# All sixteen gate pairs by seven products: the first pair's operands and sums made in another order and by other engines

## The chip, the cores and the metric

The kernel runs on one core of one Trainium2 chip. The metric is the time that the device takes for one launch, in microseconds; shown is the median of several runs. A profile of one execution shows what each engine of the core did: TensorE (PE in the profile), VectorE (DVE), ScalarE (ACT), GpSimd (POOL) and SyncE (SP), and PEld, TensorE's loading of weights, which overlaps its matmuls. ACT and DVE compute, POOL here mostly starts data transfers (DMAs) and adds a little, SP only starts transfers.

## The reference, cut to what matters

One layer of a hybrid model is computed for 640 tokens (512 of a sample, 128 of a prompt) of width 1024, all in fp32. The part that the change touches is the gated sum of four mixers:

```python
    proj = h @ lw['w_in']
    ...
    y_a = a_b * dwconv3(a_c * a_x, lw['conv_a_w'], lw['conv_a_b'])
    y_b, s_f, s_b = hgrn2_bidir(b_q, b_ff, b_fb, b_i, b_g, ...)
    y_c = ... neighbourhood_attention(qh, kh, vh, ctx_k, ctx_v, lw['na_rpb'])   # prompt: plain attention
    y_d = chunk_gmlp(d_u, d_v, lw['gmlp_norm_g'], lw['gmlp_ws'], lw['gmlp_b'])
    g_a, g_b, g_c, g_d = jnp.split(jax.nn.sigmoid(h @ lw['w_gate'] + lw['b_gate']), N_BRANCH, axis=-1)
    merged = (g_a * (y_a @ lw['w_br_a']) + g_b * (y_b @ lw['w_br_b'])
              + g_c * (y_c @ lw['w_br_c']) + g_d * (y_d @ lw['w_br_d']))
    return merged @ lw['w_o'], kh, vh, s_f, s_b
```

`h` is 640 x 1024, each `y` is 640 x 256, `w_gate` is 1024 x 4096 and each `w_br` 256 x 1024. After it come the norm and a feed-forward part of width 2816 with a short convolution.

## The kernel before, in words

**Numbers.** An fp32 operand is kept as two rounded parts, a high one (made by ACT, a copy that rounds) and a low one (made by DVE, the operand less its high part). A product is three matmuls: high by high, high by low, low by high. Features lie on the 128 partitions and tokens on the free axis, in two halves of 320 columns (`HC`), so that the matmul of most of the program is 128 x 128 by 128 x 320.

**Stages.** In this order: the modulation vectors, the input projection tile by tile, and, mixed into its matmuls, the mixers d (gMLP), b (HGRN), a (convolution) and c (attention); then the gate stage; then `w_o`, the norm, the feed-forward's up part and its down part.

**Who goes when.** The mixers and the preparation of operands are generators ("jobs"). Each `yield x` puts the job off by x of a clock that advances with the matmuls placed (`tick`), so numbers such as those in the list `HD` set how far one step of a mixer stands from the next in PE's row. `drain(f)` runs the jobs until `f` holds. Within an engine, instructions then go in the order in which they were placed; an instruction that waits holds up all behind it. From `g_all` on that order is fixed by hand (`omm`, `oact`, `ovec`, `opool` are PE, ACT, DVE and POOL with the order kept). Most such instructions have one line in the profile, that of the helper that records them (L151 before, L150 after), so they are told apart by their tiles.

**The gate stage.** It has 32 output tiles, four mixers by eight tiles of 128 features. Tiles n and n+4 of a mixer make a pair. A pair is a product of a 2 x 2 arrangement of weight blocks with a 2 x 2 arrangement of `h` (feature halves by token halves), and can be done in two ways. Plain (`gate_tile`): each tile has 48 matmuls by `h` and 12 by `y`, 120 for the pair. By seven products (Strassen's scheme, in the form with few sums): `gprod(o, p, i)` is product i, 12 matmuls, `bprod` its counterpart on `y`, 3 matmuls; 7 x 12 + 7 x 3 = 105 for the pair. Products 1 to 4 take the four quarters of `h` (kept in XH, XL0, XL1), products 5, 6 and 7 sums and differences of the quarters (kept in X1, X0 and F in some order). The weights of the seven are called A (products 1, 2), B (5, 6), Z (7) and C (4, 3); B, Z and a part of C are sums of blocks, made by DVE from two loads of `w_gp` (`raw`, and `G` or `raw`). Every operand, sum or not, has to be split into high and low. Some products add onto the bank of an earlier one, so that DVE or ACT must have taken the earlier value out before.

Before the change the first pair (mixer d, tiles 0 and 4) is plain, and the fifteen others go by seven products (`g_pair`). While the two plain tiles run on PE, the jobs make the `h` sums, the sums of the first seven-product pair's weights and their splits; the attention runs to its end in the same stretch.

**Names the steps use.** `m` and `g` are PSUM banks; `ga`, `gb` the two gates' partial sums; `y` the partial sums of the products by `y`; `g_split` splits an `h` sum, `g_zh` and `g_zl` are the high and low part of Z; `y_sums` and `y_split` make the sums of a mixer's `y` quarters and split them; `gp_load` starts the two loads of a pair's weights; `hss` are small row sums of the HGRN norm, to which POOL applies a power; `usum` and `wsum` are sums of feed-forward weights that POOL forms with accumulating transfers in DRAM, all through the middle of the program.

## Time and profile before

| | |
|---|---|
| median of 3 runs | 997.26 us (997.17 to 997.35) |
| profiled execution, its own time | 997.34 us |
| its span, first to last instruction | 995.5 us |
| mean granted TensorE clock | 0.998 |
| PE busy | 984.3 us, 7452 instructions |
| DVE busy | 864.0 us |
| ACT busy | 588.4 us |
| POOL busy | 186.6 us |
| first pair by seven products starts | 291.55 us |

The page gives the busy time of each engine over the span; the chain of waits gives, for the work that ended last, the engine on which each stretch of it lay. Rows of the timeline read: start, duration, engine, line, operation, output <- inputs, shapes, count, and in brackets the idle time before the row and what ended it. A row "x12" is twelve instructions in a row. The clock is the share of full speed that was granted to TensorE.

### The profile page before, as it was taken

Reading aid. Unit: us, or ns where it says so; the run is one execution under the profiler, and the core shown is the slowest. Engines: PE = TensorE matmul, PEld = TensorE weight load, DVE = VectorE, ACT = ScalarE, POOL = GpSimd, SP = SyncE. Lnnn points to the kernel's source line nnn. Section 1 sums busy time; section 2 is a strip of 40 time slices with the busy share of each in tenths; the row PEclk is TensorE's granted clock in tenths of the full one; section 3 lists DMA queues with packets and bytes.
Section 4 is the critical chain, followed back from the end, with each engine's and each line's share of the span. In section 5 each row is a group of like instructions: output and inputs, shape, how many; then the busy total and the mean of one; then the engine's idle time right before and its main releaser. Section 6 shows DMA issues by size and latency. Waiting matters only on the chain.

```text
span 995.5 us, 18982 instructions
## 1 busy us (share of the span) xinstructions
PE 984.3 (99%) x7452; PEld 933.1 (94%) x7452; DVE 864.0 (87%) x1413; ACT 588.4 (59%) x1018; POOL 186.6 (19%) x251
## 2 busy tenths in 40 slices
PE   8999999999999999999999999999999999999997
PEld 6899999999999999999998899999999999888886
DVE  6679899878799889898878688999999998999796
ACT  6652343455566565555656377877777777756672
POOL 1000020313112130342320021322222222100004
PEclk9999999999999999999999999999999999999999
DMA  9887343499466898999999684766666666976842
GB/s 353 338 282 249 127 134 123 133 266 273 107 223 171 235 226 291 272 225 295 290 249 367 217 324 134 221 172 167 177 170 163 177 170 193 367 262 211 288 129 106
DMA packets 74281, 220.99 MB, mean 222 GB/s; under 512 B 10192, under 2 KB 25328, under 8 KB 71504
## 3 DMA queue, kind: packets, MB, share of 16 engines
q1 hardware_dynamic: 44544, 150.96, 43.1%
q0 software_dynamic: 29648, 68.82, 29.8%
q8 instruction: 58, 0.95, 0.4%
q14 instruction: 31, 0.25, 0.1%
HBM read 176.74 MB, written 54.80 MB: 233 GB/s over the span
## 4 chain that ended last, share of the span: by engine, by line
PE 95%; DVE 2%; DMA 2%; POOL 1%; issue 1%; SPq 0%; POOLq 0%; ACT 0%
PE m L151 22%; PE g L1670 21%; PE g L375 14%; PE m L2133 9%; PE m L1670 5%; PE g L151 5%; PE m L1432 4%; PE g L2133 4%; PE g L950 2%; PE g L1432 1%; PE m L539 1%; PE m L1665 1%; DMA A<-in_w_ada_dram 1%; PE m L879 1%; POOL hss L318 1%; PE m L950 1%
## 5 line engine op out<-in xcount | busy, mean ns | idle before, releaser
L375 PE MATMUL g<-XH,w 128*128 128x320 f32 x640 | 155.0, 317 | 0.0
L375 PEld LDWEIGHTS g<-XH,w 128*128 128x128 f32 x640 | 109.5, 188 | 2.5 <-issue 1.2
L375 PE MATMUL g<-XL,w 128*128 128x320 f32 x320 | 98.8, 309 | 0.0
L151 PE MATMUL m<-XH,w 128*128 128x320 f32 x400 | 94.7, 311 | 0.0
L151 PEld LDWEIGHTS m<-XH,w 128*128 128x128 f32 x400 | 68.1, 188 | 1.2 <-ACT XH L151 0.6
L151 PE MATMUL m<-XL,w 128*128 128x320 f32 x200 | 60.6, 310 | 0.0
L375 PEld LDWEIGHTS g<-XL,w 128*128 128x128 f32 x320 | 60.3, 188 | 0.0
L2133 PE MATMUL m<-w,XH 128*128 128x512 f32 x246 | 58.5, 390 | 0.0
L2133 PEld LDWEIGHTS m<-w,XH 128*128 128x128 f32 x246 | 46.1, 188 | 9.6
L151 ACT ACTIVATE w<-raw 128x640 fp32r<-128x640 f32 (+3 forms) x54 | 49.8, 938 | 5.4 <-PE g L375 2.2
L151 DVE TENSOR_TENSOR w<-raw,w 128x640 fp32r<-128x640 f32 (+3 forms) x46 | 47.0, 1039 | 1.3 <-ACT w L151 1.2
L151 POOL DMA_DIRECT2D wsum<-in_w_dn_dram x36 | 37.0, 1211 | 48.7 <-issue 34.3
L151 PE MATMUL m<-X,w 128*128 128x320 f32 x264 | 42.3, 309 | 0.0
L151 DVE SCALAR_TENSOR_TENSOR X<-X,p2t,X 128x641 f32<-128x641 f32 x44 | 38.9, 884 | 0.9
L151 PEld LDWEIGHTS m<-X,w 128*128 128x128 f32 x264 | 39.6, 188 | 0.0
L151 DVE SCALAR_TENSOR_TENSOR X<-MG,p2t,X 128x641 f32<-128x641 f32 x44 | 38.9, 883 | 0.8
L1670 PE MATMUL g<-XL,w 128*128 128x320 f32 x240 | 38.7, 310 | 0.1
L1670 PE MATMUL g<-XL,C 128*128 128x320 f32 x240 | 38.3, 309 | 0.0
L151 PEld LDWEIGHTS m<-XL,w 128*128 128x128 f32 x200 | 37.1, 188 | 0.6 <-issue 0.6
L151 ACT ACTIVATE gb<-m 128x320 f32<-128x320 f32 x30 | 13.1, 438 | 40.7 <-PE m L151 40.7
L1670 PEld LDWEIGHTS g<-XL,w 128*128 128x128 f32 x240 | 35.9, 188 | 1.0 <-ACT MG L2030 0.5
L1670 PEld LDWEIGHTS g<-XL,C 128*128 128x128 f32 x240 | 36.0, 188 | 0.0
(611 smaller groups left out, 2864.8 us busy)
## 6 DMA issues: line engine op xcount, KB each, us to landing
wsum<-in_w_dn_dram POOLq DMA_DIRECT2D x30, 512.0 KB, 11.8
raw<-in_w_gp_dram SPq DMA_DIRECT2D x23, 640.0 KB, 6.5
raw<-in_w_up_dram SPq DMA_DIRECT2D x28, 512.0 KB, 5.0
raw<-in_w_in_dram SPq DMA_DIRECT2D x19, 512.0 KB, 4.4
H<-in_w_adt_dram SPq DMA_DIRECT2D x19, 512.0 KB, 4.0
G<-in_w_up_dram SPq DMA_DIRECT2D x12, 512.0 KB, 5.2
raw<-wsum SPq DMA_DIRECT2D x12, 512.0 KB, 5.5
actx<-X POOLq DMA_DIRECT2D x22, 256.0 KB, 4.9
```

Of the source, the lines that this page charges most:

```text
L151: r = f(*args, **kw)
L318: pool.tensor_tensor(out, out, neghalf[:, 0:n], ALU.pow)
L375: mm(o, w[:, h, k0 + k, :], r(k)[:, s], start=(k == 0 and i == 0), stop=(k == kt - 1 and i == 2))
L539: mm(m[W * g:W * g + W, (i - s0) * W:(i - s0 + 1) * W], lhs, rhs, start=True, stop=True, tile_position=(64 * par, W * g))
L879: mm(mo[64 * hh_:64 * hh_ + 64, 0:P], v, ptt[(u + hh_) % 4][:, j * P:(j + 1) * P], start=(j == 0), stop=(j == 2))
L950: mm(o, x(kx)[:, ts], w[:, h, k, :], start=(kx == 0 and i == 0), stop=(kx == 7 and i == 2))
L1432: mm(m, mh[MHN[q]][:, hx, k % 2, t * P:(t + 1) * P], wo[q][:, hw, k % 2, :], start=(k == 0 and i == 0), stop=(k == 7 and i == 2))
L1665: mm(o, w[:, k, :], x[:, k, :], start=(first and not part and k == 0 and j == 0), stop=(part == 1 and k == 3), skip_group_check=True)
L1670: z = mm(o, w[:, k, :], x[:, k, :], start=(first and k == 0 and j == 0), stop=(k == 3 and j == 2), skip_group_check=True)
L2133: mm(ps, s[t // 4][:, hx, k, o:o + P], w[:, hw, k, c0:c1], start=first, stop=i == 2 and bi == len(batch) - 1 and k == len(ks) - 1, skip_gr ...
```

## The change

All sixteen pairs go by seven products; the plain `gate_tile` and its weight tensor are dropped. A new `g_pair0` writes out the first pair's products and everything that ACT, DVE and POOL do among them, including the preparation of pair 1. To have operands ready at that time, other work moves:

- The `h` differences are made earlier, one pace apart, and the `h` sums are split into F (product 6), X1 (5) and X0 (7) as the attention lets go of those tiles; the attention's spare tiles move to other places.
- The sums of the first two pairs' weight blocks are no longer made by DVE: POOL forms them in a DRAM tensor `gsum` with twelve transfers of 320 KB, six of them accumulating, right after the HGRN state copies. The operands are then loaded from `gsum` by SP (pair 0) and POOL (pair 1).
- The gMLP's output is also stored to DRAM by POOL (`ydd`) and loaded back by SP into G, where DVE makes its sums.
- The attention's steps stand 0.9 less apart in placed matmul time (`HD[11]`), its transposed-probability copies all go to ACT, the bias reloads and the store of the result go to POOL.
- The second half of pair 1's weights is loaded into G late, by POOL, when G is free of the `y` sums.
- The merged tiles take region C in place of MG1, and the `y` operands the reverse.

```diff
-HD = [4, 5, 2.1, 7, 2.2, 1.4, 1.5, 5, 2.0, 2, 11]
+HD = [4, 5, 2.1, 7, 2.2, 1.4, 1.5, 5, 2.0, 2, 11, 0.9]
...
-NPL = 1
...
+        pool.dma_start(ydd, yt)
...
         vw = x0[:, 0:1792]
-        spt = [x0[:, 1792:2560], x1[:, 0:768]]
+        pb = region("MG1", [P, 2560])
+        spt = [x0[:, 1792:2560], pb[:, 1536:2304]]
         sps4 = [spt[i // 2][:, 384 * (i % 2):384 * (i % 2) + 384] for i in range(4)]
-        eb = [x1[:, 768:1152], x1[:, 1152:1536]]
-        mk = x1[:, 1536:2304]
-        ktk = x1[:, 2304:2560]
-        pb = region("MG1", [P, 2560])
+        eb = [x1[:, 0:384], x1[:, 384:768]]
+        mk = x1[:, 768:1536]
+        ktk = bm[:, 512:768]
...
-                    nc.sync.dma_start(eb[hh_], a["rpbe"][2 + hh_])
+                    pool.dma_start(eb[hh_], a["rpbe"][2 + hh_])
...
-            copy(ptt[u % 4], m[:, 0:384], hh_)
+            act(ptt[u % 4], m[:, 0:384], AF.Copy)
...
-            mo = pm()
+            mo = R["mo"] if "mo" in R else pm()
...
+            else:
+                R["last"] = True
+            yield HD[6] + HD[8] + HD[11]
         s3(14)
-        nc.sync.dma_start(o_ck[0, 0].rearrange("h s d -> s h d"), ktk.rearrange("p (h d) -> p h d", h=4))
-        nc.sync.dma_start(ycd, yc.bitcast(F32))
+        opool.dma_start(ycd, yc.bitcast(F32))
...
-    def gate_tile(bi, n, w):
-        br = BR[bi]
-        ps = pg()
-        gemm(ps, w, 0, 8, xhk, xlk)
-        gt = gp.tile([P, T], F32, tag="gt", name=nm("gt"))
-        gc = C_BG + GI[br] * 8 + n
-        act(c2(gt), ps[:, :, 0:HC], AF.Sigmoid, bias=p1[:, gc:gc + 1])
...
-            yield 10
+        a21, a22, a11 = d[:, 0], d[:, 1], g
+        for x, h, c in ((a21, 0, 1), (a22, 1, 1), (a11, 0, 0)):
+            yield 4
             nc.sync.dma_start(x, hdr[h, c])
-        while "scores" not in R or "ada39" not in R:
+        yield 6
...
+            yield 6
...
+        def place(i, x, t):
...
+        while "r" not in gx:
+            yield 0.5
+        r = gx["r"]
+        s = gw[0, "S"] = [gp.tile([P, 5, P], F32, tag="gt", name=nm("s")) for i in range(2)]
+        for i in range(2):
+            nc.sync.dma_start(s[1 - i], gsum[0][:, 1 - i])
+        g_s23(0, r)
+        while "ab0" not in R:
+            yield 0.5
+        lows = g_c(0, r)
+        low(*lows[0])
+        while "ab1" not in R:
+            yield 0.5
+        b = gw[0, "B"] = gunit(0, 1)
+        for i in range(2):
+            oact(b[:, 0, 1 - i], s[1 - i], AF.Copy)
+        low(b[:, 1, 1], s[1], b[:, 0, 1])
+        while "scores" not in R:
+            yield 0.5
+        place(6, a11, "F")
+        R["gx3"] = True
+        yield 1
+        place(5, a22, "X1")
+        low(b[:, 1, 0], s[0], b[:, 0, 0])
+        yield 0.5
+        ovec.tensor_tensor(a22, a12, a11, ALU.add)
+        g_zh(0, r)
+        gx["t3"] = a22
+        gx["Y"] = a11.rearrange("p a t -> p (a t)")
+        y_load(0)
+        low(*lows[1])
+        while "yc" not in R:
+            yield 0.5
+        place(7, a21, "X0")
+        gx["Y1"] = a21.rearrange("p a t -> p (a t)")
...
+        if bi == 0:
+            nc.sync.dma_start(gx["Y"], ydd)
+            return
...
+    gsum = dram.tile([2, P, 3, 5, P], F32, name="gsum")
...
+        if p_ != 1:
+            gp_load2(p_, r)
+        return r
+    def gp_load2(p_, r):
+        if p_ > 1:
+            nc.sync.dma_start(r[1], gp_raw(p_, 1))
+        else:
+            eng = opool if p_ else nc.sync
+            eng.dma_start(r[1][:, 0], gp_raw(p_, 1)[:, 0])
+            eng.dma_start(r[1][:, 1], gsum[p_][:, 2])
...
+        if p_ == 1:
+            opool.dma_start(gx["S"], gsum[1][:, 0:2])
+            return
...
+    def g_pair0(r):
+        gx["bi"] = 0
+        bank = [pm() for i in range(4)]
+        R["mo"] = bank[2]
+        b1, b3, b2, b4 = [m[:, 0:HC] for m in bank]
+        ga = gw[0, "gt", 0] = gp.tile([P, T], F32, tag="gt", name=nm("ga"))
+        gb = gw[0, "gt", 1] = gp.tile([P, T], F32, tag="gt", name=nm("gb"))
+        ps = gw[0, "ps"] = pg()
+        p1_, p3_ = ps[:, 1, 0:HC], ps[:, 0, 0:HC]
+        gprod(b1, 0, 1, True)
+        oact(ga[:, 0:HC], b1, AF.Copy)
+        bprod(p1_, 0, 1, True)
+        oact(p3_, p1_, AF.Copy)
+        gprod(b4, 0, 4, True)
+        gprod(b3, 0, 2, True)
+        ovec.tensor_tensor(ga[:, 0:HC], b3, ga[:, 0:HC], ALU.add)
+        g_sig(0, 0, ga[:, 0:HC], ga[:, 0:HC])
+        bprod(p3_, 0, 2, False)
+        gprod(b1, 0, 6, False)
+        oact(gb[:, 0:HC], b1, AF.Copy)
+        drain(lambda: "t3" in gx)
+        g_split(3, gx["t3"])
+        g_s01(1, r[1])
+        drain(lambda: "Y1" in gx)
+        gprod(b2, 0, 5, True)
+        g_zl(0, r[0])
+        g_a(1, r[1])
+        gprod(b1, 0, 7, False)
+        oact(gb[:, HC:T], b1, AF.Copy)
+        y_sums()
+        ovec.tensor_tensor(ga[:, HC:T], b4, gb[:, HC:T], ALU.add)
+        g_sig(0, 0, ga[:, HC:T], ga[:, HC:T])
+        ovec.tensor_tensor(gb[:, HC:T], b2, gb[:, HC:T], ALU.subtract)
+        gx["C"] = region("MG1", [P, 2, 3, HC], F32R)
+        lows, x3 = y_split()
+        oact(x3[2], x3[1], AF.Copy)
+        for x in lows + [x3]:
+            low(*x)
+        gp_load2(1, r[1])
+        g_al(1, r[1])
+        gprod(b2, 0, 3, False)
+        y = gw[0, "y"] = gp.tile([P, T], F32, tag="gt", name=nm("y"))
+        c2_ = gw[0, "b2"] = pm()[:, 0:HC]
+        bprod(p1_, 0, 6, False)
+        oact(y[:, 0:HC], p1_, AF.Copy)
+        bprod(c2_, 0, 5, True)
+        ovec.tensor_tensor(gb[:, 0:HC], b2, gb[:, 0:HC], ALU.subtract)
+        bprod(p1_, 0, 7, False)
+        oact(y[:, HC:T], p1_, AF.Copy)
+        ovec.tensor_tensor(y[:, HC:T], c2_, y[:, HC:T], ALU.subtract)
+        late = []
+        g_b(1, late)
+        g_s23(1, r[1])
+        late += g_c(1, r[1])
+        r[2] = gp_load(2)
+        g_zh(1, r[1])
+        for x in late:
+            low(*x)
+        gx["Y"] = gx["Y1"]
...
-        drain(lambda: "gx3" in R)
+        drain(lambda: "gx3" in R and "last" in R)
...
+        g_pair0(r)
+        for p_ in range(1, GPAIR + 1):
+            for _ in range(5):
...
+        while "stc" not in R:
+            yield 1
+        for o, h, i, add in ((0, 0, 0, 0), (2, 1, 0, 0), (0, 1, 1, 1), (2, 1, 1, 1), (1, None, 0, 0), (1, 1, 0, 1)):
+            for p_ in range(2):
+                bi, n = gp_id(p_)
+                g = gsum[p_][:, i] if h is None else gp_raw(p_, h)[:, i]
+                z = pool.dma_start(gsum[p_][:, o], g, accum_op=ALU.add) if add else pool.dma_start(gsum[p_][:, o], g)
+                tc.keep_in_program_order(z)
+                yield 0.7
```

The table of instructions that results differs at three places that matter below.

**PE, from the first pair's end of product 1 to pair 1's second product.** Before, with product 2's last matmul, then 6, b2, 5, 7, b6, b5 (`m_358` is the bank of products 1, 6, 7 and 4, `m_364` that of 5 and 3):

```order
L151 MATMUL m_359_3726<-XH_14_256,w_334_3519 128x320
L151 MATMUL m_358_3725<-X0_346_3642,w_349_3664 128x320 x12
L151 MATMUL g_362_3743<-E_249_2778,w_334_3519 128x320 x3
L151 MATMUL m_364_3792<-X1_344_3625,w_349_3664 128x320 x12
L151 MATMUL m_358_3725<-F_339_3575,S0_351_3683 128x320 x12
L151 MATMUL g_362_3743<-C_357_3724,w_349_3664 128x320 x3
L151 MATMUL m_366_3819<-C_357_3724,w_349_3664 128x320 x3
```

After, with product 2's last matmul, then b2, 6, 5, 7 and the first two rows of product 3 (`m_341` is the bank of 1, 6 and 7, `m_343` that of 5 and 3):

```order
L150 MATMUL m_342_3581<-XH_14_258,w_313_3314 128x320
L150 MATMUL g_347_3586<-E_249_2793,w_313_3314 128x320 x3
L150 MATMUL m_341_3580<-F_339_3575,w_338_3571 128x320 x12
L150 MATMUL m_343_3582<-X1_348_3590,w_338_3571 128x320 x12
L150 MATMUL m_341_3580<-X0_350_3605,S0_349_3601 128x320 x12
L150 MATMUL m_343_3582<-XH_14_258,w_332_3488 128x320
L150 MATMUL m_343_3582<-XL0_15_259,w_332_3488 128x320
```

Product 3 has moved up to stand right behind product 7, on the bank that product 5 filled; products 6, 5 and 7 stand together, with b2 ahead of them; product 4 has moved ahead of product 2, and b6, b5 and b7 behind product 3; then pair 1's product 1 begins.

**DVE around the split of the second `h` quarter's low part (`XL0`) and the low part of Z (`S0`).** Before:

```order
L151 TENSOR_TENSOR S0_351_3683<-raw_310_3261,S0_351_3683 128x640
L151 TENSOR_TENSOR XL0_15_257<-D_269_2885,XH_14_256 128x4x320
L151 TENSOR_TENSOR ga_360_3727<-m_359_3726,ga_360_3727 128x320
L151 TENSOR_TENSOR D_269_2885<-D_269_2885 128x320 x4
```

After:

```order
L150 TENSOR_TENSOR ga_345_3584<-m_342_3581,ga_345_3584 128x320
L150 TENSOR_TENSOR XL0_15_259<-D_269_2901,XH_14_258 128x4x320
L150 TENSOR_TENSOR S0_349_3601<-raw_288_3058,S0_349_3601 128x640
L150 TENSOR_TENSOR G_270_2902<-G_270_2902 128x320 x4
L150 TENSOR_TENSOR ga_345_3584<-m_344_3583,gb_346_3585 128x320
L150 TENSOR_TENSOR gb_346_3585<-m_343_3582,gb_346_3585 128x320
```

The low part of Z now stands behind the low part of the `h` quarter, and the bank of product 5 (`m_343`) is taken out behind a sum that needs product 7 (`gb`).

**ACT in the first pair and at the start of pair 1.** After the change, from the first sigmoid to the copy of product 7 (the two rows `gb<-m_341` are the copies of products 6 and 7 out of their bank):

```order
L150 ACTIVATE ga_345_3584<-ga_345_3584,cst_81 128x320
L150 ACTIVATE gb_346_3585<-m_341_3580 128x320
L150 ACTIVATE XH_14_258<-D_269_2901 128x4x320
L150 ACTIVATE B_351_3674<-raw_340_3578 128x1280
L150 ACTIVATE gb_346_3585<-m_341_3580 128x320
```

The split of the `h` quarter (`XH<-D`) now stands behind the copy of product 6, where before it stood behind product 1's. Further on, up to the copy of pair 1's product 1 (`m_363<-m_362`):

```order
L150 ACTIVATE w_357_3737<-raw_340_3578 128x640
L150 ACTIVATE w_357_3737<-G_353_3703 128x640
L150 ACTIVATE S0_349_3601<-G_353_3703 128x640
L150 ACTIVATE gb_346_3585<-gb_346_3585,cst_81 128x640
L150 ACTIVATE m_363_3758<-m_362_3757 128x320
```

`G_353`, read by two splits ahead of `m_363`, is the half of pair 1's weights that POOL now loads late, where before SP had loaded it ahead of the pair.

158 lines of the change are left out of this document (44 added, 114 removed).

## The prediction

> **What bounds the kernel now.** I read the page first, then the chain of waits, then the busy time in stretches.
>
> ```profile
> PE 984.3 (99%) x7452; PEld 933.1 (94%) x7452; DVE 864.0 (87%) x1413; ACT 588.4 (59%) x1018; POOL 186.6 (19%) x251
> ...
> PE 95%; DVE 2%; DMA 2%; POOL 1%; issue 1%; SPq 0%; POOLq 0%; ACT 0%
> ```
> ```profile
> 200.00:300.00 100.00, 99.85 (x761) 94.23 (x760) 81.31 (x161) 54.10 (x100) 21.61 (x29) 1.00 0.75 218
> 300.00:400.00 100.00, 100.00 (x684) 100.00 (x683) 89.28 (x122) 60.02 (x98) 22.10 (x33) 1.00 0.80 231
> ```
>
> TensorE is busy 99% of the span, and 95% of the chain lies on it. In the stretch of the change (200 to 300 us) it idles 0.15 us in 100; between 300 and 400, all gate products, never. So two things follow. A matmul that goes is worth its full pitch, and there is no idle time to win beyond that. Any new wait on TensorE is lost in full, since nothing behind it has slack for it to be made up. The pitch: 684 matmuls in 100 us, 0.1462 us each.
>
> **What is removed.** The plain pair has 120 matmuls, seven products have 105. 15 x 0.1462 = 2.19 us. That is the most that the change can give: 997.34 (the profiled execution) - 2.19 = 995.15 us. DVE, ACT and POOL do about the same amount as before; nothing on the path gets shorter by it.
>
> **What is moved, around the first pair.** What hides the work of ACT and DVE is the run of matmuls in front of the product that needs it. Before, up to 291.55 us two plain tiles are that cover:
>
> ```profile
> 289.79 1.92 PE L375 MATMUL g<-E,w 128*128 128x320 f32 x12
> 291.55 0.31 PE L151 MATMUL m<-XH,w 128*128 128x320 f32 x1
> ...
> 293.57 0.44 ACT L151 ACTIVATE ga<-m 128x320 f32<-128x320 f32 x1 [0.45 <-PE m L151]
> ...
> 294.03 0.82 DVE L151 TENSOR_TENSOR S<-raw,S 128x640 fp32r<-128x640 f32 x1
> ...
> 294.34 1.26 ACT L151 ACTIVATE XH<-D 128x1280 fp32r<-128x1280 f32 x1
> ...
> 295.51 1.92 PE L151 MATMUL m<-X,w 128*128 128x320 f32 x12
> 295.64 1.49 DVE L151 TENSOR_TENSOR XL<-D,XH 128x1280 fp32r<-128x1280 f32 x1 [0.79 <-ACT XH L151]
> ...
> 297.27 0.60 PE L151 MATMUL g<-E,w 128*128 128x320 f32 x3
> ...
> 299.47 1.92 PE L151 MATMUL m<-F,S 128*128 128x320 f32 x12
> ...
> 301.23 0.60 PE L151 MATMUL g<-C,w 128*128 128x320 f32 x3
> 301.43 0.44 ACT L151 ACTIVATE gb<-m 128x320 f32<-128x320 f32 x1 [1.31 <-PE m L151]
> ...
> 302.53 0.48 DVE L151 TENSOR_TENSOR gb<-m,gb 128x320 f32<-128x320 f32 x1
> ```
>
> Twelve matmuls take 1.76 us (295.51 to 297.27), three 0.44. A copy out of a bank starts 0.20 us after the product's last matmul (301.23 to 301.43) and takes 0.44. The low part of Z (`S<-raw,S`, 0.82) is done at 294.85, 4.6 us ahead of product 7 (299.47). The split of the `h` quarter (`XH`, 1.26, then `XL`, 1.49) is needed only after product 7. After the change the plain tiles are gone: the first pair starts about 120 x 0.1462 = 17.5 us earlier, at 291.55 - 17.5 = 274.0, and the chains below stand closer to the products that need them. I call the end of product 6 E6.
>
> *Product 7.* It needs the low part of Z from its third matmul on. In DVE's new row that stands behind the low part of the `h` quarter, which waits for the quarter's high part on ACT, which stands behind the copy of product 6. So from E6: 0.20 + 0.44 (copy; the next starts some 0.04 early) + 1.26 (`XH<-D`) + 0.05 + 1.40 (the pitch of a DVE operation of 1.49) + 0.82 (`S`) + 0.08 = about 4.2 us. Cover: product 5 (1.76) and two matmuls (0.29), 2.05. TensorE waits **2.1 us**. All of it is from rows; the bounds are 1.8 and 2.5.
>
> *Product 3.* It adds onto product 5's bank, so it waits until DVE has taken that out. The subtraction stands behind the sum that uses the copy of product 7. From the end of product 7: 0.20 + 0.44 + 0.04 + 0.40 + 0.48 + 0.08 = 1.64 us, and not one matmul lies between. **1.65 us**; bounds 1.4 and 2.0. Before, products b6 and b5, the whole of product 4 and b7 lay between.
>
> *Small ones.* Product b2 waits for ACT's copy of b1's bank, delayed by the splits ahead of it: 0.18. Product b7 waits for the copy of b6 (0.20 + 0.44 + 0.08) with b5 (0.44) between: 0.26. Pair 1's product 1 waits for the low part of its weights, the last of DVE's row of splits: 0.3. Together **0.7**, bounds 0 and 1.5.
>
> **The late half of pair 1's weights.** POOL starts its two loads of 320 KB into G once DVE has read the last of the `y` sums there. ACT must split both (0.42 to 0.74 us each, rows like `w<-raw`), then compute a sigmoid of 640 (0.82), then copy pair 1's product 1, for which TensorE's next product waits. Times: E6 = 274.0 + 54 matmuls (7.9) + 0.55 (next paragraph) + 0.2 = 282.65; product 7 ends at 282.65 + 4.2 + 1.45 = 288.3, product 3 at 288.3 + 1.65 + 1.76 = 291.7; b6, b5, b7, product 1, and the nine matmuls before the wait bring TensorE to 296.7. After product 7 DVE and ACT have 0.2 + 0.44 + 0.4 + 0.5 for the gates, a sigmoid and then the three splits of `y`; G is free at about 292.2, and the second load is issued about 293.1. It lands L later; ACT then has 0.74 + 0.82 + 0.44, and TensorE goes on at 295.1 + L. The wait is L - 1.6. No load of this size from POOL is in the trace. The nearest:
>
> ```profile
> raw<-in_w_gp_dram SPq DMA_DIRECT2D x23, 640.0 KB, 6.5
> ...
> usum<-in_w_up_dram POOLq DMA_DIRECT2D x18, 256.0 KB, 10.2
> ...
> usum<-usum POOLq DMA_DIRECT2D x6, 256.0 KB, 5.7
> ...
> C<-F POOLq DMA_DIRECT2D x9, 256.0 KB, 3.4
> ```
> ```profile
> 290.00:295.00 5.00, 5.00 (x36) 5.00 (x35) 3.39 (x5) 3.58 (x6) 0.00 (x0) 1.00 0.92 305
> ```
>
> 3.4 us is a light load, 10.2 one among many others in flight. Here the DMA engines were 0.92 busy in the same stretch; after the change the next pair's loads go out at about this time too. I take 5.0, between 3.4 and the 6.5 of twice the size: a wait of **3.4 us**, bounds 1.8 and 8.6. [...]
>
> **The attention.** Its steps move 0.9 closer.
>
> ```profile
> 229.32 0.56 DVE L2311 COPY MG<-m 128x384 f32<-128x384 f32 x1 [0.53 <-PE m L862]
> ...
> 235.88 0.41 DVE L859 TENSOR_SCALAR X<-X,ast 128x384 f32<-128x384 f32 x1
> ```
> ```profile
> 270.51 1.48 DVE L1067 TENSOR_TENSOR D<-D 128x1280 f32<-128x1280 f32 x1
> 275.61 1.49 DVE L1067 TENSOR_TENSOR D<-G,D 128x1280 f32<-128x1280 f32 x1
> ```
> ```profile
> 230.00:260.00 30.00, 30.00 (x244) 27.80 (x241) 26.16 (x61) 13.55 (x31) 10.30 (x13) 1.00 0.79 214
> ```
>
> DVE has 3.84 us free between 230 and 260. Five steps take 4.5 us out of that; three differences of 1.4 come in (270 and later before), and up to eight copies of 0.56 go to ACT. 4.5 + 4.2 - 4.5 - 3.84 = 0.4. Following DVE's row step by step, its scaling (0.41) for the sixth pair of units ends at 260.15 while TensorE wants it at 259.6. I take **0.55**, bounds 0 and 1.5. Where TensorE waits there, 40 matmuls in front have already been used as cover.
>
> **The POOL sums** cost nothing:
>
> ```profile
> 146.17 2.24 POOL L572 COPY D<-st_in 64x128 f32<-64x128 f32 x4
> 187.23 1.01 POOL L318 TENSOR_TENSOR hss<-hss,neghalf 128x4 f32<-128x4 f32 x1 [38.81 <-DVE hss L317]
> ```
>
> POOL is idle from 148.4 to 187.2. Twelve transfers at 0.6 to 1.0 us of issue, and three waits for a landing in a row, each 5.7 (the accumulating `usum<-usum`), end by 148.4 + 10 + 17 = 175. With 10.2 each: 189, 2 us late, on a row that the chain of waits runs through. So 0, bound 2.
>
> **The sum.** -2.19 + 2.1 + 1.65 + 0.7 + 3.4 + 0.55 = +6.2. On the profiled execution 997.34 + 6.2 = 1003.5; the median of the runs is 0.08 below it, so about **1003.5 us**.
>
> **Rivals.**
> 1. *Only the matmuls count* (995.2 us). ACT and DVE would need to be 4 us ahead of what their rows give. DVE idles 1.6 of 5 us at 290, which is for it; the order of the instructions is against.
> 2. *The late load is early* (L under 2, or ACT not behind it): 1003.5 - 3.4 = 1000.1. For it: the queue of POOL is short there. Against: the busy DMA engines.
> 3. *The waits are half of what I say*, +2 against -2.19: 997.2, no change.
> 4. *The late load is the bound*, slower: L of 8 to 10 gives +9 to +11, 1006 to 1008.5.
> 5. *The clock falls.* If TensorE stands still long enough, its clock is taken down:
>
> ```profile
> 987.76 1.17 PE L2133 MATMUL m<-w,MG 128*128 128x192 f32 x9
> ```
> ```profile
> 991.00:991.50 0.50, 0.00 (x0) 0.00 (x0) 0.44 (x1) 0.44 (x1) 0.03 (x1) 1.00 0.65 254
> 991.50:992.00 0.50, 0.00 (x0) 0.00 (x0) 0.32 (x1) 0.28 (x1) 0.00 (x0) 0.71 0.00 0
> ```
>
> The last matmul ends at 988.93, and the clock falls about 2.9 us later. A wait of 3.4 us could do the same; if the clock needs as long to come back, 2.9 us at half speed lose 1.5: 1005.0 us. [...]
>
> **How the numbers follow.** The forecast 0.40 (1001.5 to 1005.5), rival 1 0.05, rival 2 0.20, rival 3 0.16, rival 4 0.11, rival 5 0.08. The range, 998.5 to 1007.5, leaves out rival 1, most of 3 and the upper part of 4, some 0.2. A change under 0.2% (2.0 us) cannot be told from none: faster 0.05, within 0.19 (rival 3 and a small part of 2), slower 0.76 (rival 2 falls mostly there, at 0.28%).
>
> **What would show it.** In the profile after: TensorE's first idle time within the gate stage, ended by DVE's `S` (2.1 us, in product 7), by DVE's `gb` (1.65, ahead of product 3) and by ACT's `m` behind `w<-G` (3.4); a lower busy share of TensorE between 255 and 300 and the same 100% later; 15 matmuls fewer. No `S` wait would mean that the order of DVE's row is not what it seems; a wait ended by `hss` that the POOL sums do cost. A faster kernel with these waits in it would mean that time is won in a place that I have not seen.

## The result, and the profile after

The change makes the kernel slower: 1005.70 us (median of 4 executions, 1005.43 to 1006.26) against 997.21 us of the kernel before on the same chip, a ratio of 1.0086 [1.0068, 1.0103]. The profiled execution took 1005.73 us, 8.4 us more than that of before; its span is 1003.8 us and its mean granted clock 0.995, where before it was 0.998.

The page, engines and chain of waits:

```profile
PE 987.3 (98%) x7437; PEld 934.4 (93%) x7437; DVE 864.7 (86%) x1413; ACT 592.6 (59%) x1034; POOL 195.5 (19%) x267
...
PE 90%; DVE 5%; DMA 2%; issue 1%; POOL 1%; ACT 1%; SPq 0%; POOLq 0%; DVEq 0%; ACTq 0%
```

The 15 matmuls are gone (7452 before, 7437 now), and yet TensorE's busy time rose by 3.0 us: the work has not grown, so some of it ran more slowly, and the granted clock below shows where. TensorE's share of the chain fell from 95% to 90%.

Busy time in stretches of 100 us (PE, PEld, DVE, ACT, POOL, then the granted clock, the share of the DMA engines and GB/s):

```profile
200.00:300.00 100.00, 94.17 (x701) 86.88 (x700) 80.23 (x160) 56.34 (x113) 24.03 (x34) 0.98 0.64 198
300.00:400.00 100.00, 99.81 (x670) 99.81 (x671) 84.41 (x114) 57.36 (x93) 26.02 (x36) 0.98 0.91 253
```

The damage is between 200 and 304 us: 5.9 us of idle time that were not there before (6.02 in the two rows, against 0.15), and a clock of 0.98 in both rows, which was 1.00. The 0.98 of the second row lies in its first four microseconds, as a finer view will show. What TensorE waited for there (total, times, longest, from the waits view of TensorE):

```profile
PE m L150 <- DVE S L150: 1.9, 1, 1.9
PE m L150 <- ACT m L150: 1.8, 1, 1.8
PE m L150 <- DVE gb L150: 1.7, 1, 1.7
```

These are the three waits that the prediction names. In time order on TensorE, where the last bracket is the idle time and what ended it:

```profile
280.93 1.92 PE L150 MATMUL m<-F,w 128*128 128x320 f32 x12
282.68 1.92 PE L150 MATMUL m<-X,w 128*128 128x320 f32 x12
284.44 0.46 PE L150 MATMUL m<-X,S 128*128 128x320 f32 x2
286.80 3.00 PE L150 MATMUL m<-X,S 128*128 128x320 f32 x10 [1.90 <-DVE S L150]
291.53 0.39 PE L150 MATMUL m<-XH,w 128*128 128x320 f32 x1 [1.74 <-DVE gb L150]
...
300.19 0.41 PE L150 MATMUL m<-XH,B 128*128 128x320 f32 x1 [1.84 <-ACT m L150]
...
303.30 2.21 PE L150 MATMUL m<-F,w 128*128 128x320 f32 x12
```

Products 6 and 5 run through (1.92 us as displayed for twelve, starts 1.75 apart). Product 7 does two matmuls, stops, and does its other ten in 3.00 us; at full clock ten show 1.73 (e5). On DVE, ACT and POOL the causes:

```profile
283.22 1.26 ACT L150 ACTIVATE XH<-D 128x1280 fp32r<-128x1280 f32 x1
```
```profile
284.51 1.49 DVE L150 TENSOR_TENSOR XL<-D,XH 128x1280 fp32r<-128x1280 f32 x1 [2.82 <-ACT XH L150]
285.92 0.82 DVE L150 TENSOR_TENSOR S<-raw,S 128x640 fp32r<-128x640 f32 x1
...
290.30 0.49 DVE L150 TENSOR_TENSOR ga<-m,gb 128x320 f32<-128x320 f32 x1 [1.58 <-ACT gb L150]
290.89 0.49 DVE L150 TENSOR_TENSOR gb<-m,gb 128x320 f32<-128x320 f32 x1
```
```profile
294.52 0.55 POOL L150 DMA_DIRECT2D G<-gsum  x1
```
```profile
G<-gsum POOLq DMA_DIRECT2D x1, 320.0 KB, 3.7
```
```profile
295.32 0.44 ACT L150 ACTIVATE y<-g 128x320 f32<-128x320 f32 x1 [0.81 <-PE g L150]
295.65 1.26 ACT L150 ACTIVATE w<-D 128x1280 fp32r<-128x1280 f32 x1
297.10 0.74 ACT L150 ACTIVATE w<-raw 128x640 fp32r<-128x640 f32 x1 [0.19 <-DVE raw L150]
297.75 0.72 ACT L150 ACTIVATE w<-G 128x640 fp32r<-128x640 f32 x1
298.38 0.72 ACT L150 ACTIVATE S<-G 128x640 fp32r<-128x640 f32 x1
299.00 0.81 ACT L150 ACTIVATE gb<-gb,cst 128x640 f32<-128x640 f32 x1
299.72 0.41 ACT L150 ACTIVATE m<-m 128x320 f32<-128x320 f32 x1
```

The low part of Z (`S`) ends at 286.74 and product 7 goes on at 286.80. The subtraction that frees product 5's bank ends at 291.38 and product 3 goes on at 291.53. The late load is issued at 294.52 and lands 3.7 us later, at 298.22. ACT splits it at 298.38, computes the sigmoid and makes the copy for which TensorE waits until 300.19. But ACT did not stand waiting for that load: from its copy of product b7 (`y<-g`, 295.32) on it works with one break of 0.19 us, and `S<-G` follows `w<-G` by 0.63 us, as closely as where a load has long landed (297.34 behind 296.71 in e1).

TensorE's busy time and the granted clock (the number behind the busy time), in stretches of 3.41 us laid where the clock changes:

```profile
283.46:286.87 3.41, 1.51 (x11) 1.00 0.19 77
286.87:290.28 3.41, 2.92 (x10) 0.50 0.68 203
290.28:293.69 3.41, 2.16 (x15) 1.00 0.45 182
293.69:297.10 3.41, 3.26 (x22) 1.00 0.54 168
297.10:300.51 3.41, 1.57 (x11) 1.00 0.89 245
300.51:303.92 3.41, 3.41 (x15) 0.50 1.03 300
```

Twice the clock is 0.50 for 3.41 us, from 286.87 and from 300.51, each time after 3.41 us in which TensorE was busy 44% (1.51 of 3.41) or 46% (1.57). After 63% (2.16) and 96% (3.26) it was 1.00. Neither wait is longer than 1.9 us.

### The profile page after: what moved, and what is told of

It reads as the page before. It is cut to its first block, busy times and chain, and to the rows that moved or that the text cites. A ratio compares the mean times of both kernels' runs of the same rounds, so it can differ in the third digit from the quotient of the medians.

```text
span 1003.8 us, 18999 instructions
## 1 busy us (share of the span) xinstructions
PE 987.3 (98%) x7437; PEld 934.4 (93%) x7437; DVE 864.7 (86%) x1413; ACT 592.6 (59%) x1034; POOL 195.5 (19%) x267
## 4 chain that ended last, share of the span: by engine, by line
PE 90%; DVE 5%; DMA 2%; issue 1%; POOL 1%; ACT 1%; SPq 0%; POOLq 0%; DVEq 0%; ACTq 0%
PE m L150 23%; PE g L1721 21%; PE g L374 11%; PE m L2184 8%; PE m L1721 5%; PE g L150 5%; PE m L1474 4%; PE g L2184 4%; PE g L955 2%; PE g L1474 1%; PE m L539 1%; PE m L1716 1%; DMA A<-in_w_ada_dram 1%; POOL hss L317 1%; PE m L955 1%
## 5 line engine op out<-in xcount | busy, mean ns | idle before, releaser
L374 PE MATMUL g<-XH,w 128*128 128x320 f32 x576 | 140.6, 318 | 0.0
L374 PEld LDWEIGHTS g<-XH,w 128*128 128x128 f32 x576 | 98.7, 188 | 2.4 <-issue 1.2
L150 PE MATMUL m<-XH,w 128*128 128x320 f32 x416 | 98.4, 311 | 1.7 <-DVE gb L150 1.7
L374 PE MATMUL g<-XL,w 128*128 128x320 f32 x288 | 89.0, 309 | 0.0
L150 PEld LDWEIGHTS m<-XH,w 128*128 128x128 f32 x416 | 70.8, 188 | 3.5 <-ACT ga L150 2.1
L150 PE MATMUL m<-XL,w 128*128 128x320 f32 x208 | 63.0, 310 | 0.0
L374 PEld LDWEIGHTS g<-XL,w 128*128 128x128 f32 x288 | 54.2, 188 | 0.1
L1721 PE MATMUL g<-XL,w 128*128 128x320 f32 x240 | 38.6, 310 | 0.0
L1721 PEld LDWEIGHTS g<-XL,w 128*128 128x128 f32 x240 | 36.0, 188 | 0.6 <-ACT MG L150 0.3
L150 PE MATMUL m<-X,S 128*128 128x320 f32 x192 | 32.3, 318 | 1.9 <-DVE S L150 1.9
L150 PE MATMUL m<-XH,B 128*128 128x320 f32 x128 | 31.9, 318 | 1.8 <-ACT m L150 1.8
```

The costliest lines, as they stand in the source:

```text
L150: r = f(*args, **kw)
L374: mm(o, w[:, h, k0 + k, :], r(k)[:, s], start=(k == 0 and i == 0), stop=(k == kt - 1 and i == 2))
L1721: z = mm(o, w[:, k, :], x[:, k, :], start=(first and k == 0 and j == 0), stop=(k == 3 and j == 2), skip_group_check=True)
```

## The experiments

Times are medians, with lowest and highest; ratios are to the kernel before, run between them on the same chip, whose median was 997.1 to 997.3 each time. The theory at the outset was the prediction's: three chains of ACT and DVE work stand too close to the products that need them. From the profile after came a second part: the waits also bring the clock down, to 0.50 behind two of the three. The reorderings keep the computation; where an experiment does extra work it is said. The executions of e1 to e3 lie 1.8 to 5.1 us apart and their intervals overlap, so their medians alone do not decide between theory and rival; there the rows of the profiled executions do.

### e1: the low part of Z made early

In the first pair's preparation instead of behind the split of the `h` quarter:

```diff
         low(*lows[1])
+        g_zl(0, r)
...
         gprod(b2, 0, 5, True)
-        g_zl(0, r[0])
```

> The low part of Z (DVE's S, 0.82 us) of the first pair is made earlier, right after its high part, instead of behind the low part of the h quarter (XL). Nothing else changes. In the changed kernel TensorE waits 1.9 us for it in product 7 (2.07 from the last matmul's pitch), and the granted clock then stands at 0.50 from 286.87 to 290.27, which costs product 7 another 1.4 us. Theory: the waits stand in a chain. Product 7 ends at 286.2 instead of 289.6, but DVE is then still at the y sums until 288.0, and the two operations ahead of product 3 end only at 288.9, so the wait there grows from 1.7 to about 2.7 us; with it TensorE is idle for more than half of the stretch 286.87 to 290.27, and the clock is down in the next such stretch. The late load keeps its wait of 2. Gain about 1.0 us: 1004.7. Rival (the waits are independent): the wait and the slow matmuls both go, 2.07 + 1.4 less: 1002.3.

Measured: 1004.05 us (1001.97 to 1005.88, 4), ratio 1.0068 [1.0049, 1.0087]. TensorE in its profile (span 1000.7):

```profile
289.16 0.60 PE L150 MATMUL m<-XH,w 128*128 128x320 f32 x1 [2.77 <-DVE gb L150]
...
299.15 0.41 PE L150 MATMUL m<-XH,B 128*128 128x320 f32 x1 [1.83 <-ACT m L150]
```
```profile
292.14 0.55 POOL L150 DMA_DIRECT2D G<-gsum  x1
```
```profile
294.28 0.44 ACT L150 ACTIVATE y<-g 128x320 f32<-128x320 f32 x1 [0.80 <-PE g L150]
...
297.34 0.72 ACT L150 ACTIVATE S<-G 128x640 fp32r<-128x640 f32 x1
```

The wait for `S` is gone, so DVE's order was its cause. But the wait for `gb` grew from 1.74 to 2.77, and the third is unchanged: 1.0 of the 1.9 us came back at the next place. The third wait also shows that the late load does not make it. The load was issued 2.38 us earlier than in after (292.14), took 3.6 us and landed at 295.74, 1.6 us before ACT read it, and TensorE still waited 1.83 us. From ACT's copy of product b7 to TensorE's restart there are 4.87 us in both kernels (294.28 to 299.15, 295.32 to 300.19): ACT's own row sets the wait, and it starts from a product of TensorE. The clock fell once in this execution (0.50 from 288.74 to 292.15, after a stretch with 1.06 of 3.41 us busy), not twice; at the end of the late wait the kernel is 1.04 us ahead of after, at its end 3.1.

### e2: product 5 taken out of its bank at once

DVE copies product 5 out, so that product 3 need not wait for the sum with product 7:

```diff
+        y = gw[0, "y"] = gp.tile([P, T], F32, tag="gt", name=nm("y"))
+        ovec.tensor_copy(y[:, HC:T], b2)
...
-        ovec.tensor_tensor(gb[:, HC:T], b2, gb[:, HC:T], ALU.subtract)
+        ovec.tensor_tensor(gb[:, HC:T], y[:, HC:T], gb[:, HC:T], ALU.subtract)
```

> Product 5's value is copied out of its bank by DVE during product 7 (one more DVE operation of some 0.5 us, into a part of y that is free), and the difference that stood between product 7 and product 3 reads the copy. So product 3 no longer waits for ACT's copy of product 7 and two DVE operations; 1.9 us from product 7's end to product 3's start go away there. Theory (chain): product 6's counterpart on y then waits for the split of the y sums, which ends at the same time as before (DVE's MG at 292.7), so 1.2 of it come back at once, and the rest is lost at the late load, whose landing (298.2) and the ACT row behind it set the restart at 300.2 as before: no gain, 1005.6. Rival (independent waits): 1003.8.

Measured: 1004.20 us (1003.39 to 1005.15, 4), ratio 1.0070 [1.0055, 1.0085]. In its profile the wait for `gb` is gone, and the late wait ends where it did:

```profile
300.06 0.42 PE L150 MATMUL m<-XH,B 128*128 128x320 f32 x1 [1.78 <-ACT m L150]
```

300.06 against 300.19: of 1.74 us, 0.13 was kept in this execution. The span is 0.4 shorter than that of after (this execution took 1005.15 us, the longest of the four). So the three waits are not three independent costs. What sets the restart here is a chain that begins at the end of product 7 and goes through the splits of `y` and of pair 1's weights on ACT and DVE, beside product 3 and not through it. The load adds at most 0.15 us to it: it lands at 298.1, and `S<-G` starts 0.78 us behind `w<-G` in place of 0.63. (The median, 1004.20, lies nearer to the rival's 1003.8; two of the four executions, 1003.39 and 1004.36, have a mean clock of 0.999, the profiled one 0.995, so the clock is mixed into it.)

### e3: ACT's copies ahead of the splits

Pair 1's C and Z are split behind ACT's copies, not ahead of them:

```diff
-        late += g_c(1, r[1])
         r[2] = gp_load(2)
-        g_zh(1, r[1])
...
         oact(p3_, p1_, AF.Copy)
+        if not q:
+            c_lows = g_c(1, r[1])
+            g_zh(1, r[1])
```

> ACT's splits of pair 1's C weights and Z (w<-raw, w<-G, S<-G, 2.2 us, two of them behind the late loads) and their DVE counterparts are placed behind ACT's copies of pair 1's first products instead of ahead of them. TensorE's second product of pair 1 then waits for a sigmoid and a copy only. Theory: the restart moves from 300.2 to about 298.2, and with TensorE busy from 297.1 to 300.5 the clock stays at 1.00 after it, which saves the 1.6 us that product 2 and the next lost at 0.50: 2.0 + 1.6 less, 1002.1. Rival (the slow matmuls come from the transfers in flight, DMA share about 1.0 there, not from the idle time): 1003.7. Rival (the splits are then late for products 7 and 4 of pair 1): 1005 or more.

Measured: 1003.58 us (1001.62 to 1006.76, 4), ratio 1.0067 [1.0046, 1.0087]. The wait for `m` is gone, so its cause was ACT's order: the copy stood behind the splits. The profiled execution is the fastest of the four, 1001.62 us, and it has the first two waits as in after, without a fall of the clock:

```profile
286.77 1.75 PE L150 MATMUL m<-X,S 128*128 128x320 f32 x10 [1.89 <-DVE S L150]
290.25 0.39 PE L150 MATMUL m<-XH,w 128*128 128x320 f32 x1 [1.74 <-DVE gb L150]
```

Ten matmuls take 1.75 here and 3.00 in after, behind the same wait. With four executions 5.1 us apart, this kernel cannot be told from e1 and e2 by its median.

### e4: TensorE kept busy in the first wait

Fourteen matmuls that compute nothing that is used, ahead of product 7:

```diff
+        for k in range(14):
+            omm(b3, gw[0, "A"][:, 0, 0, k % 4, :], gx["x"][1][0][:, k % 4, :], start=True, stop=True,
+                skip_group_check=True)
         gprod(b1, 0, 7, False)
```

> Fourteen extra matmuls (128x320, on operands that are there, into a bank that nobody reads any more) are placed between product 5 and product 7 of the first pair, 2.05 us, as long as the wait in product 7. The wait for DVE's S ends when it did, 286.8; what changes is that TensorE isn't idle before it. Theory (the clock is taken down by idle time): the clock stays at 1.00 from 286.87 on, product 7 takes its usual 1.5 us for ten matmuls instead of 2.8, everything behind it up to the late load is 1.4 earlier, G is free 1.4 earlier, the load lands 1.4 earlier: 1004.3 us with 14 matmuls more. Rival (the slow matmuls have another cause, such as the engines working beside it): no gain, 1005.7, or up to 2 more if the extra matmuls delay.

Measured: 1005.66 us (1004.96 to 1005.82, 4), ratio 1.0083 [1.0066, 1.0100]: no gain. Product 7 ran at full clock and product 3 began at 290.52, 1.0 earlier than in after; the late wait ended at 299.17, also 1.0 earlier. But the clock still fell behind the late wait (0.52 from 299.8 to 303.2 us), and a wait of 1.0 us for DVE's `w` that after does not have came up behind the gate stage. The microsecond won did not last to the end. That the clock stayed up in product 7 fits idle time as its cause, but does not show it: in e3 and e11 the same wait, not filled, brought no fall either in the profiled execution. Extra idle time alone is tried in e7, e8 and e12.

### e5 and e6: all reorderings together, and the attention's spacing

e5 has e1 to e3 in one, and more: the sums of `y` go ahead of the low part of the last `h` quarter, the splits of `y` ahead of the copy of product 7, and B's splits and the first pair's sigmoids behind pair 1's product 1. e6 also sets the attention's steps a little wider:

```diff
+        y_sums()
+        ovec.tensor_tensor(l3, gx["t3"], h3.bitcast(F32), ALU.subtract)
...
         g_al(1, r[1])
+        gprod(b1, 0, 7, False)
+        oact(gb[:, HC:T], b1, AF.Copy)
...
         oact(p3_, p1_, AF.Copy)
+        if not q:
+            late = []
+            g_b(1, late)
...
-HD = [4, 5, 2.1, 7, 2.2, 1.4, 1.5, 5, 2.0, 2, 11, 0.9]
+HD = [4, 5, 2.1, 7, 2.2, 1.4, 1.5, 5, 2.0, 2, 11, 1.1]
```

> All waits of the first pair taken up at once, by order alone: the low part of Z early; the y sums ahead of the low part of the h quarter on DVE; product 5's value copied out during product 7; the splits of the y sums ahead of product 7's copy, so that G is free and the late loads go out some 5 us earlier (issue 288.5 instead of 294.0); ACT's and DVE's splits of pair 1's B, C and Z weights behind ACT's copies of pair 1's first products. Theory (the waits stand in a chain, each hidden by the one before it, and the low clock follows from them): what is left is the attention's 0.6, b2's 0.1, b7's 0.3, pair 1's products 1 and 6 with up to 0.3 each; -2.2 + 1.6 = about 996.6 us (996.0 to 997.5), no stretch of low clock, and runs that agree within 0.5 us. Rival: the order only moves the waits on to pair 1's products 6, 7 and 4, whose weights are then late: 999 to 1002, with low clock.

> The kernel of e5 with the attention's steps 0.2 farther apart (HD[11] 1.1 instead of 0.9). Theory: DVE gets 1 us more between the steps, the 0.2 to 0.35 us that TensorE waits for its scaling at 260.4 go, and the attention still ends within the projection's matmuls: 0.3 under e5. Rival: the attention's last steps then come behind the last of the projection's matmuls with nothing to cover them, each waiting for ACT and DVE: 1 to 3 us over e5.

Measured: e5 1002.55 us (1001.24 to 1003.91, 5), ratio 1.0050 [1.0037, 1.0062]; e6 1000.38 us (999.68 to 1001.89, 7), ratio 1.0033 [1.0022, 1.0043]. My theory for e5, that the waits add up and go together, is wrong by 6 us. The rival, that they move on to pair 1's products, is right for four of the five waits below, though not in the low clock that it expected. TensorE in e5:

```profile
287.85 0.39 PE L150 MATMUL m<-XH,w 128*128 128x320 f32 x1 [0.92 <-DVE y L150]
297.87 1.73 PE L150 MATMUL m<-F,w 128*128 128x320 f32 x10 [0.97 <-DVE w L150]
302.49 1.73 PE L150 MATMUL m<-X,S 128*128 128x320 f32 x10 [0.40 <-DVE S L150]
305.77 0.41 PE L150 MATMUL m<-XH,w 128*128 128x320 f32 x1 [0.67 <-ACT gb L150]
308.76 0.41 PE L150 MATMUL m<-XH,w 128*128 128x320 f32 x1 [0.53 <-DVE gb L150]
```

Five new waits, 3.49 us together, none over 1 us, and no fall of the clock in the gate stage. In e6 product 6 begins 0.73 earlier (280.76, 281.49 in e5), and the waits for `y` and `S` shrink to 0.36 and nothing. e6 is 2.2 us faster than e5 by the medians, where its theory had 0.3. The earlier start and the 0.96 us less of waits account for 1.7; the rest is not placed, and it is not the clock, whose mean is 0.998 or 0.999 in every execution of both.

### e7, e8 and e12: the cost of one wait alone

In the kernel before, which never waits there, ACT makes 4, 9 or 6 extra copies (results overwritten) ahead of one copy that TensorE needs at 402 us:

```diff
+        for _ in range(4 if p_ == 7 else 0):      # 9 in e8, 6 in e12
+            oact(ga[:, 0:HC], b1, AF.Copy)
         oact(b3 if q >= 0 else ga[:, 0:HC], b1, AF.Copy)
```

> The kernel before, with four extra copies of 0.40 us on ACT ahead of the copy of one late pair's product 1 (its eighth by seven products), so that TensorE waits there about 1.0 us longer than the nine matmuls in between cover. It changes no result. It measures what an idle stretch costs by itself. [...] Rival (any wait of about a microsecond takes the clock down): 999.9.

> As e7 with nine extra copies: an idle stretch of about 3.0 us. [...]

> The kernel before, with six extra copies on ACT ahead of the copy of pair 7's product 1, so that TensorE stands still once, for about 1.95 us (four extra copies gave 1.01, nine 3.35: 0.47 each), as long as each of the three waits of the changed kernel. [...] So two groups of executions: about 999.4 (997.26 + 1.95 + 0.15 for the restart) without a fall and about 1000.7 with one (the fall after nine copies cost 2.09 + 1.95 - 0.6 - 2.1 = 1.3), each with at least a quarter of the executions. Rival 1: a wait of 2 us never makes the clock fall unless the DMA and the other engines are as in the changed kernel: all within 0.5 us of 999.4. Rival 2: it always does: all within 0.5 us of 1000.7.

By estimate, a fall as in after (3.41 us at 0.50) loses 1.7 us. So e7 comes to 997.2 + 1.0 = 998.2 us without a fall, and e8 to 997.2 + 3.0 = 1000.2 without and 1001.9 with one.

(In e12's text the working behind 1.3 us is garbled; it is 1002.09 - 997.26 - 3.35 - 0.15 = 1.33, from e8.) TensorE's one wait in e7, e12 and e8, in this order:

```profile
402.67 0.41 PE L151 MATMUL m<-XH,w 128*128 128x320 f32 x1 [1.01 <-ACT m L151]
```
```profile
403.55 0.42 PE L151 MATMUL m<-XH,w 128*128 128x320 f32 x1 [1.94 <-ACT m L151]
```
```profile
404.93 0.42 PE L151 MATMUL m<-XH,w 128*128 128x320 f32 x1 [3.35 <-ACT m L151]
```

| wait, us | executions, us | over 997.2, less the wait |
|---|---|---|
| 1.01 (e7) | 10 from 998.11 to 999.05, median 998.43 | 0.2 |
| 1.94 (e12) | 999.09, 999.29; 1000.61, 1000.65, 1000.78; 1001.94 | 0.1; 1.5; 2.8 |
| 3.35 (e8) | 4 from 1001.94 to 1002.79, median 1002.09 | 1.5 |

A wait of 1 us costs itself, one of 3.35 us cost some 1.4 more in each execution, and one of 1.94 us costs it in some executions and not in others. The two groups that e12's text names are there, 1.5 us apart, in one kernel; each rival allowed but one. The mean clock of each execution agrees: 0.997 and 0.998 in the lower group, 0.996 in all three of the upper. That second sign is needed, since the kernel before has executions 1.1 to 1.5 us above its median too (4 of 19 beside e9, 998.45 to 998.84), with a mean clock of 0.998 or 0.999. (The single execution at 1001.94 stands outside both groups; it was not profiled, its mean clock is 0.997, so a second fall does not explain it, and I have no cause for it.) The profiled execution of e12 is the one of 999.09, without a fall. In e8 the clock's stretches are:

```profile
402.10:405.50 3.40, 0.57 (x4) 1.00 0.89 291
405.50:408.90 3.40, 3.40 (x15) 0.51 1.09 306
408.90:412.30 3.40, 3.40 (x25) 0.99 1.24 199
```

17% busy, then 3.4 us at 0.51 with 15 matmuls where the next stretch has 25. TensorE had stood still for 3.35 us and was back at work 0.57 us before the clock fell. A fixed time behind the last matmul does not give the fall: ahead of the wait the last one ended at 401.6, almost 4 us before it, and at the end of the kernel before the fall came after 2.8.

What decides between a fall and none behind the same wait was not shown. The profiled execution of e11 has the three waits of after (1.90, 1.74 and 1.83 us), and its clock stayed. TensorE's busy time and clock in e11, and below them in after:

```profile
284.00:288.00 4.00, 2.10 (x14) 1.00 0.44 138
288.00:292.00 4.00, 2.26 (x16) 1.00 0.74 297
```
```profile
284.00:288.00 4.00, 2.10 (x12) 0.86 0.15 15
288.00:292.00 4.00, 2.26 (x10) 0.72 0.82 314
```

The busy times are the same and the clocks are not. In the 3.41 us ahead of a fall TensorE was busy 17 (e8), 31 (e1), 44 and 46 (after) and, in e2, 48% (1.63 us, ahead of its second fall); the clock was 1.00 behind 51% in e1 (1.75 of 3.41 us) and behind 63 and 96% in after.

### e9, e10 and e11: the remaining waits, and the spacing alone

e9 is e6 with the last `h` quarter split ahead of product 6's copy and pair 1's B split ahead of ACT's copy of pair 1's product 1 (against after, cut):

```diff
         gprod(b3, 0, 2, True)
+        drain(lambda: "t3" in gx and "Y1" in gx)
+        h3, l3 = gx["x"][3]
+        oact(h3, gx["t3"], AF.Copy)
...
+        gw["late"] = []
+        g_b(1, gw["late"])
+        g_s23(1, r[1])
```

e10 is e9 with 1.3 for the spacing; e11 is after with 1.1 and nothing else.

> All reorderings of e6, and the two waits of close to 1 us that e6 still shows are taken away by order alone: ACT and DVE split the last quarter of h (XH, XL) ahead of product 6's copy and ahead of the y sums, and they split pair 1's B (the w that product 6 of pair 1 waits 0.97 us for) ahead of ACT's copy of pair 1's product 1. Theory: the change's 15 matmuls are worth 2.19 us, and what stands against them is waits alone and the clock that falls for them; with e6's waits of 0.97 (w) and 0.36 (y) gone and 0.67, 0.53, 0.21 left, the time is e6's 1000.4 less 1.3 to 1.8, so 998.6 to 999.1, and as low as 996.5 if ACT gb's 0.67 and DVE gb's 0.53 are also met earlier; no two neighbouring 3.41-us stretches are left half idle, so the clock doesn't fall and runs agree within 1 us. Rival: ACT and DVE simply have too much to do between 280 and 305 us, so a wait that is taken away at one place comes back at the next product: 1000.0 to 1001.0, with new waits that sum to as much as in e6 (2.7 us).

> As e9, with the attention's steps set 1.3 apart in place of 1.1 (after: 0.9). Theory: spacing beyond 1.1 only moves the attention's steps to later places in TensorE's row, and its end waits for the same chain of ACT and DVE; same as e9 within 0.5 us. Rival: wider spacing hides the rest of the attention's waits, as from 0.9 to 1.1, where product 6 of the first pair began 0.73 us sooner: 0.5 to 1.0 us faster than e9. Second rival: the steps now come too late and the first pair's operands with them: 1 us slower than e9.

> The changed kernel with one number changed: the attention's steps 1.1 apart in place of 0.9, so that spacing is seen without any reordering. Theory: between e5 and e6, which differ by the same number, product 6 of the first pair began 0.73 us sooner and the rest of the 2.2 us was the clock, which in some executions no longer fell; here the waits of 1.9, 1.7 and 1.8 us that make it fall are still there, so 1005.7 less 0.7: 1005.0. Rival: the spacing itself is worth the 2.2 us: 1003.5.

Measured:

| | median, us | lowest to highest, executions | ratio |
|---|---|---|---|
| e9 | 998.67 | 997.60 to 999.13, 11 | 1.0011 [1.0002, 1.0020] |
| e10 | 999.59 | 998.83 to 1001.52, 9 | 1.0025 [1.0015, 1.0035] |
| e11 | 1004.83 | 1003.29 to 1005.97, 4 | 1.0075 [1.0061, 1.0089] |

e9 is where the theory puts it (998.6 to 999.1), with executions 1.5 us apart and TensorE's named waits in the gate stage down to these:

```profile
293.23 0.42 PE L150 MATMUL m<-XH,B 128*128 128x320 f32 x1 [0.33 <-ACT m L150]
304.96 0.41 PE L150 MATMUL m<-XH,w 128*128 128x320 f32 x1 [0.53 <-DVE gb L150]
```

So the rival, a fixed amount of ACT and DVE work that must come out somewhere, falls: of the loss of 8.5 us, 7.2 were order, with the spacing and with the clock, which is 1.00 in e9's rows below. What is left eats up the 2.19 us. The same stretches as above, in e9:

```profile
200.00:300.00 100.00, 99.07 (x749) 92.50 (x748) 84.59 (x166) 58.66 (x117) 27.54 (x39) 1.00 0.70 215
300.00:400.00 100.00, 99.35 (x676) 98.83 (x675) 86.34 (x118) 58.62 (x96) 21.89 (x31) 1.00 0.92 250
```

TensorE idles 1.58 us in the two, 0.15 before, and that is no longer the clock. At the first matmul of `w_o` e9 stands at 522.86, before at 522.10: 2.95 us lost against the 2.19, of which 1.43 are idle time; each restart takes some 0.2 more until matmuls are at their pitch again (0.17 in product 7 of after), and the rest I have not placed. e9 does not beat the kernel before.

In e10 TensorE waits 1.02 us for ACT's copy of a `g` bank ahead of product 6, which begins at 281.66; ACT's row ahead of that copy stands 1.1 later than in e9 (its split `S<-raw` at 278.51 after a wait for DVE's `D`, in e9 at 277.38). The wider spacing makes the first pair's operands late: the second rival. e11's median agrees with its theory (1005.0), but its interval, 1003.4 to 1006.2, holds the rival's 1003.5 too. The theory's premise, that between e5 and e6 the rest was the clock, does not hold, as said there. The profiled execution of e11 is its fastest, and shows once more what the clock is worth: it has the three waits of after (shown above), the clock stayed at 1.00 from 280 to 308 us, and it took 1003.29 us, 2.4 less than the profiled execution of after, of which 0.42 is the spacing (product 6 begins at 280.51, in after at 280.93; the theory had 0.7). Here the clock is worth less than in the account below, since e11 waits 1.07 us late in the program (for DVE's `gcol` at 917.72), where after waits 0.24.

## Why the prediction was right, and where its sum was not

The direction, the places of the three waits and what ends the first two were right, and 1005.7 lies in the range, though just outside the forecast's own 1001.5 to 1005.5. What makes the third wait was wrong. The sum was too low by 2.2 us, and behind that stand two terms off in opposite directions. From the rows of after against before, up to the first matmul of `w_o` (530.24 against 522.10, 8.1 us later; only some 0.2 more is lost behind it):

| step of the prediction | predicted, us | measured, us |
|---|---|---|
| 15 matmuls less | -2.19 | -2.2 |
| product 7, wait for `S` | +2.1 | +2.07 |
| product 3, wait for `gb` | +1.65 | +1.90 |
| small ones | +0.7 | +0.5 |
| late load | +3.4 | +2.0, set by ACT's row and not by the load |
| attention | +0.55 | +0.58 |
| POOL sums | 0 | 0 |
| clock | not in the sum | +3.0 |
| sum | +6.2 | +7.9 |

A wait measured so includes the restart (1.90 idle and 0.17). The start of the program took 0.1 less; so 0.4 of the 8.1 is not placed.

*Product 7 and product 3.* The step-by-step reckoning along ACT's and DVE's new rows gave both to within 0.25 us. e1 and e2 show each cause by taking it away. What they also show is that the prediction was wrong to treat the terms as separate: e1 got back 1.0 of 2.07 and e2 0.13 of 1.90 at the point where the late wait ends. The total added up because all three stood together; the parts were not each worth their row.

*The late load.* This is the step that failed. The prediction lets the landing of the second load start ACT's row, so that the wait is L - 1.6. Its size was off: L is 3.7 us, not 5.0. I went between 3.4 for a light load and 6.5 for twice the bytes, and the DMA engines were 0.54 busy from 293.7 to 297.1 us, when the two loads set out, against the 0.92 of the stretch of before that I went by. The mechanism was off too. That issue + L + 2.0 gives the restart (294.52 + 3.7 + 2.0 = 300.2) is luck: the load landed at 298.22, and ACT came to it by its own row at 298.38. In e1 it landed 1.6 us before ACT read it, and the wait was the same. What the prediction left out is that ACT has two other splits of pair 1's weights (`w<-D`, 1.26 us, and `w<-raw`, 0.74) between its copy of product b7 and those of the late half. With them 0.20 + 4.87 us pass from the end of b7 to the restart, and 21 matmuls, 3.07 us, lie between: 2.0 us of wait, whenever the load is there in time. e3, with the copy ahead of the splits, takes the wait away.

*The clock.* This is the missing term. I had it as rival 5 only, at one fall, with a chance of 0.08, and reckoned it from the fall behind the last matmul: 2.9 us of standing still (2.8 by the clock's rows), so a wait of 3.4. That a wait has to be so long is not what the runs show: TensorE had stood still for less there (in the 3.41 us ahead of that fall it was busy 0.64), and both falls of after came on waits of 1.9 and 1.8 us, and cost 1.37 (ten matmuls of product 7 in 2.83 us, 1.46 at full clock) and 1.63 (pair 1's product 2 by 1.35, the start of product 6 by 0.28), close to the 1.5 of rival 5; the clock was back after 3.41 us, where rival 5 took 2.9. Falls are not peculiar to the profiled execution: the mean clock of the four is 0.993 to 0.996, and 0.998 or 0.999 in every execution of the kernel before beside the experiments.

*The POOL sums.* POOL issued the last of them at 171.0, and the row that the chain of waits ran through did not move (187.23 before):

```profile
187.09 1.05 POOL L317 TENSOR_TENSOR hss<-hss,neghalf 128x4 f32<-128x4 f32 x1 [14.68 <-DVE hss L316]
```

*The rivals.* Rival 1, that only the matmuls count, needed ACT and DVE 4 us ahead; e9 comes to 998.67 when they are given a better order, so even then the 2.19 us are used up. Rival 2 would have the wait go when the load is early; e1's load was early and the wait stayed. Rival 3's time does not follow from its words: half of the 8.4 us of waits is 4.2, which against 2.19 leaves +2.0 and 999.3 us, not 997.2; the waits came to 7.1 us, clock aside. Rival 4 needed 8 to 10 us and had 3.7. Rival 5 named the fall of the clock (0.50, twice in after) with too long a wait.

## What to carry to other kernels

Taking matmuls off a TensorE that never waits is worth their pitch only if the work of the other engines still fits under what is left: follow each engine's new row from one fixed event to the product that needs it, as for products 7 and 3, but reckon the waits as one chain, since the one taken away is mostly taken up by the next. A wait on TensorE such as those of 1.8 to 1.9 us here should be priced with the clock on top, some 1.4 us each in a share of the executions (1.37 and 1.63 in the profiled execution of after, 1.5 in three of the six of e12, none in the profiled one of e11), and an idle time cut into pieces of under 1 us can be cheaper than the same time in one (e5: 3.49 us in five pieces and no fall; e8: 3.35 us in one and 1.5 more). Before a wait is put down to the load at the head of an engine's row, see whether that engine stood still for it. Where executions of one kernel lie in groups, 1.5 us apart in e12, look at the granted clock of each before comparing two kernels by a few of them; the kernel before has such a group without the clock.
